# Two TensorE orders in a two-layer encoder: a differential head's outputs behind the next head's transposes, the first latent scores behind the latent values

## Chip, core and metric

The kernel runs on one core of one Trainium2 chip. Its engines work side by side, each through its own queue in order: TensorE (PE in the profile: matmuls, with the loads of their stationary operand shown apart as PEld), VectorE (DVE), ScalarE (ACT), GpSimd (POOL) and SyncE (SP), which issues the loads from memory. The metric is device time in microseconds; the time of a kernel is the median of several executions. One further execution is recorded by the hardware profiler, and all rows in this document are from such executions.

## What is computed

An encoder of two layers over 256 tokens with 2048 features, in f32. In each layer a differential attention and a latent attention stand side by side and are joined by gates; an output projection, a SwiGLU network and a gated embedding follow. The part that matters here, shortened:

```python
for i in range(DEPTH):                                   # 2 layers
    z = rmsnorm(x, g_mix[i]) @ w_in[i]
    dq, dk, dv, cq, ckv, kr, ga, gb = split(z)
    # differential attention: 8 heads, two softmax maps of 64 features each
    probs = softmax(einsum('bqhcd,bkhcd->bhcqk', rope(dq), rope(dk)) * 64 ** -0.5)
    od = (probs[:, :, 0] - lam * probs[:, :, 1]) @ dv
    y_diff = (rmsnorm(od, g_subln[i]) * (1 - lam_init)) @ w_branch_diff[i]
    # latent attention: 8 heads; queries, keys and values come from low-rank latents
    qf = rmsnorm(cq, g_q_latent[i]) @ w_q_up[i]           # 128 plain + 64 rotated features a head
    kvf = rmsnorm(ckv, g_kv_latent[i]) @ w_kv_up[i]       # 128 key + 128 value features a head
    probs = softmax((q_nope @ k_nope + rope(q_rope) @ rope(kr)) * 192 ** -0.5)
    y_mla = (probs @ v_mla) @ w_branch_mla[i]
    x = x + (sigmoid(ga) * y_diff + sigmoid(gb) * y_mla) @ w_out[i]
    x = x + swiglu(rmsnorm(x, g_ffn[i]))
    x = x + sigmoid(rmsnorm(x, g_ple[i]) @ w_ple_gate[i]) * (p[i] @ w_ple_in[i])
```

## The kernel before

Activations lie transposed, features on the 128 partitions and the 256 tokens along the free dimension, in 16 tiles. For accuracy, operands are split into a high and a low part: `split` does it for an activation (ScalarE copies the high part, VectorE subtracts, lines 250 and 251 with line 74), `piece` for up to 1024 columns of weights, which SyncE loads (line 180), ScalarE rounds to `whi` and VectorE subtracts to `wlo` (line 181). `emit` then runs, for each block of 128 input features, one matmul of `whi` with both parts of the activation (line 211, 512 columns) and one of `wlo` with its high part (line 215, 256 columns). This pair of matmuls is nearly all of the work. `joined` adds the two halves of a finished bank (ScalarE's copy on line 242, then VectorE). Weight splits have three buffers each, the loaded weights four, results of `joined` four (`a`).

PSUM, the matmuls' output memory, is given out in banks: four for projections and values (`ps_mm`, line 63), two for scores (`ps_s`, line 64), and two for all the rest (`ps_at`, line 65): transposes, head outputs, rotations, norms.

One differential head goes through these steps:

- `scores` (line 348): 12 matmuls into two score banks, one for each map;
- `exps` (lines 354 to 358): VectorE takes the maxima, ScalarE the exponentials with their sums (line 357), VectorE the reciprocals; then `diff_weights` scales and joins the two maps (lines 557 and 558) into the weights `E`;
- `turned` (line 366): four transposes of the weights into one bank, then ScalarE's copy of it to `wt` (line 368);
- `diff_out` (line 567): eight matmuls of `wt` with the values into another bank; ScalarE copies it out (line 570) and squares it twice for the norm (line 572). `settle` later scales the outputs of four heads, transposes them (line 582) and splits them.

`pipelined` lays the heads of one attention over each other and over other work. In turn h it takes a step of filling work, starts the scores of head h+1, traces head h's transposes, takes a second step, and then traces head h's outputs. For the differential heads the filling work is the generator `beside`: the queries and keys of later heads, the latent keys, the shared rotated key (with `rotated`, line 326), from head 6 on `settle` and the latent queries (`queries_up`, of which two of six pieces are rotated). What is left of it is taken after the loop, and then `values` computes the latent values (lines 399 to 401, into `mmv` banks). The latent heads go through `pipelined` too, with projections of the gates as filling work; `mla_weights` has their scores, also on line 348.

The code gives the work in an order, but the order in which each engine's queue gets it is planned when the program is built: the framework runs a model of the engines and hands each engine, at each modelled moment, the first traced instruction whose inputs and buffers are ready. Work traced later can so be drawn forward into a gap that the model sees. `tc.issue_after(x)` forbids it for one case: whatever is traced in its block on x's engine stays behind x. It orders a queue and adds no semaphore. `last_mm` holds the most recent line-401 matmul.

Of the kernel before, what the change touches and what calls it, by code (L numbers as in the profile page):

```python
# [19 lines left out]
P = 128  # L20
# [4 lines left out]
DH = 8  # L25
# [27 lines left out]
def encoder(ctx, tc, x, p, positions, cols, lams, wq, wk, wv, wcq, wckv, wkr, wga, wgb,  # L53
            w_q_up, w_kn, w_v, w_bd, w_bm, w_out, w_gate, w_up, w_down, w_pin, w_pg, rope_c, out):
    nc = tc.nc
    V, A, PE = nc.vector, nc.scalar, nc.tensor
# [13 lines left out]
    def bank(ps=ps_at, tag="at", name="at", shape=(P, 2 * T)):  # L70
        return ps.tile(list(shape), F32, tag=tag, name=name)

    def tt(o, a, b, op):
        return V.tensor_tensor(out=o, in0=a, in1=b, op=op)  # L74
# [4 lines left out]
    def ts(o, a, s1, s2, op0, op1=ALU.bypass):  # L79
        return V.tensor_scalar(out=o, in0=a, scalar1=s1, scalar2=s2, op0=op0, op1=op1)  # L80
# [29 lines left out]
    ident = const.tile([P, P], F32, name="ident")  # L110
# [83 lines left out]
    last_split, last_mm, chores, sq0, step = [], [], [], [], []  # L194
# [24 lines left out]
    def product(src, us, whole=False, inside=None):  # L219

        acc = bank(ps_mm, "mm", "mm")
        n = len(us)
        for a in range(0, n, PT):
            m = min(PT, n - a)
            hi, lo = piece(src[:, a * P : (a + m) * P], m)
            emit(acc, hi, lo, 0, us[a : a + m], a == 0, a + m == n, whole, inside and (inside[0] - a, inside[1]))
        return acc[:, :T] if whole else acc
# [10 lines left out]
    def joined(acc, o=None):  # L240
        t = scratch("join", 3)
        A.activation(t, acc[:, T:], AF.Copy)  # L242
        o = scratch("a", 4) if o is None else o
        tt(o, acc[:, :T], t, ALU.add)
        return o
# [74 lines left out]
    krs = [const.tile([P, 2 * T], F32R, name=f"kr{j}") for j in range(2)]  # L320
# [16 lines left out]
    def three(q, k):  # L337
        return [(q[:, :T], k[:, T:]), (q[:, T:], k[:, :T]), (q[:, :T], k[:, :T])]

    def scores(*maps):  # L340


        Ss = [bank(ps_s, "S", "S", (P, 2, T)) for _ in maps]
        for b in range(2):
            for j in range(len(maps[0])):
                for S, pairs in reversed(list(zip(Ss, maps))):
                    q, k = pairs[j]
                    PE.matmul(S[:, b, :], q[:, b * P : (b + 1) * P], k, start=j == 0, stop=j == len(pairs) - 1)  # L348
        return Ss

    def exps(S, E, scale):

        nm, sm, rs = (stat.tile([P, 2], F32, tag=t, name=t, bufs=4) for t in ("nm", "sm", "rsum"))
        V.tensor_reduce(out=nm, in_=S, axis=AX.X, op=ALU.max, negate=True)
        ts(nm, nm, scale, None, ALU.mult)
        for b in range(2):
            last_exp[0] = A.activation(E[:, b, :], S[:, b, :], AF.Exp, bias=nm[:, b : b + 1], scale=scale, accum_out=sm[:, b : b + 1])  # L357
        V.reciprocal(out=rs, in_=sm)
        return rs

    def turned(W, parts=False):

        tp = bank(shape=(P, 2, T))
        for kb in range(2):
            for b in range(2):
                PE.transpose(tp[:, kb, b * P : (b + 1) * P], W[:, b, kb * P : (kb + 1) * P], ident)  # L366
        wt = [tmp.tile([P, 2, T], F32R if parts else F32, tag="wt", name="wt", bufs=4) for _ in range(1 + parts)]
        A.activation(wt[0], tp, AF.Copy)
        if not parts:
            return wt[0]  # L370
        tt(wt[1], tp, wt[0].bitcast(F32), ALU.subtract)
        return wt
# [4 lines left out]
    def weights(tag="E", dt=F32):  # L377
        return tmp.tile([P, 2, T], dt, tag=tag, name=tag, bufs=2)

    last_exp = [None]  # L380
    ROPE16 = [(j + 8) if j < 8 else (j - 8) if j < 16 else j for j in range(32)]

    def values(src, us, load=None):
# [39 lines left out]
    for L in range(DEPTH):  # L423
# [43 lines left out]
        qn, kn, qr = [], [], ub[14:]  # L467
# [40 lines left out]
        def beside():  # L508

            for h in range(2, DH):  # L510
                if h < 6:
                    keys_up(2 * h - 4)
                elif h == 7:
                    rotated(joined(product(wkr[L, 0], ua)), crm, srm)
                yield
                queries_keys(h)
                yield
            settle(0)
            for n in (8, 0, 2, 10):
                queries_up(n)  # L520
                yield
            settle(4)
            for n in (4, 6):
                queries_up(n)
# [21 lines left out]
        fill = beside()  # L546
# [13 lines left out]

        def diff_out(h, W):
            wt = turned(W)
            yield
            o = bank()
            for b in range(2):
                for kb in range(2):
                    PE.matmul(o[:, b * P : (b + 1) * P], wt[:, kb, b * P : (b + 1) * P], head(vd, kb, h), start=kb == 0, stop=kb == 1)  # L567
            f = fa(h)
            od.append(f[:, 0, :])
            A.activation(od[h], o[:, :T], AF.Copy)  # L570
            for b in range(2):
                A.activation(f[:, 1, :P], od[h][:, b * P : (b + 1) * P], AF.Square, accum_out=ssd[:, 2 * h + b : 2 * h + b + 1])
# [9 lines left out]
                    PE.transpose(t[:, b * P : (b + 1) * P], o, ident)  # L582
                split(ods[h], t[:, :T], gsub[:, L : L + 1])

        def pipelined(weigh, put, heads, step):
            W = weigh(0)
            for h in range(heads):
                step()
                nxt = weigh(h + 1) if h + 1 < heads else None
                out = put(h, W)  # L590
                next(out)
                step()
                next(out, None)
                W = nxt

        pipelined(diff_weights, diff_out, DH, lambda: next(fill, None))
        for _ in fill:
            pass
        vm, = (v for v in values(w_v[L], ckv) if v is not None)
# [4 lines left out]

        def mla_weights(h):
            E = weights()
            S, = scores(three(qn[h], kn[h]) + three(qr[h // 2], krs[h % 2]))
            r = exps(S, E, MLA_SCALE)
            for b in range(2):
                ts(E[:, b, :], E[:, b, :], r[:, b : b + 1], None, ALU.mult)  # L610
            return E

        def mla_out(h, W):
            v = head(vm, slice(None), h)
            vs = weights("E1", F32R)
            vh, vl = vs[:, :, :P], vs[:, :, P:]
            A.activation(vh, v, AF.Copy)
            tt(vl, v, vh.bitcast(F32), ALU.subtract)
            wh, wl = turned(W, True)
            yield  # L620
            o = bank()
            for kb in range(2):
                for j, (a, b) in enumerate(((vh, wh), (vh, wl), (vl, wh))):
                    PE.matmul(o[:, :T], a[:, kb, :], b[:, kb, :], start=kb + j == 0, stop=kb + j == 3)  # L624
            split(oms[h], o[:, :T])

        pipelined(mla_weights, mla_out, MH, lambda: gate(wga, gate_a, next(todo)))


# [26 lines left out]
        for part, (f0, f1) in enumerate(FF_PARTS):  # L656
            for f in range(f0, f1):
# [6 lines left out]
                b = pre.pop(0) if pre else joined(product(w_up[L, f], ub))  # L664
# [128 lines left out]
```

## Time and profile before

| | us |
|---|---|
| median of 3 runs | 2852.53 (2852.42 to 2852.87) |
| the profiled execution, in all | 2853.86 |
| its span, first to last instruction | 2852.1 |
| differential heads, layers 1 and 2 | about 112 to 235 and 1525 to 1649 |
| latent heads | about 221 to 346 and 1634 to 1759 |

A row of the timeline has start, duration, engine, line, operation, output and inputs by their names in the program, the array's rows and columns for a matmul, shape, and how many were merged; in square brackets stands how long the engine was idle ahead of it and which instruction ended that. Matmuls overlap: the next starts before the last one's duration is over, so the step from start to start is what one costs. Tiles of `ps_at` are named `at`, those of the scores `S`. A row of busy times by stretch has the stretch, its length, then the busy time of PE, PEld, DVE, ACT and POOL, the granted clock, the share of time in which the DMA engines moved data, and GB/s. A row of waits has the waiting engine and line, the releasing one, us in total, how often, and the longest.

### The profile page before, as it was taken

Reading aid. Unit: us, or ns where it says so; the run is one execution under the profiler, and the core shown is the slowest. Engines: PE = TensorE matmul, PEld = TensorE weight load, DVE = VectorE, ACT = ScalarE, POOL = GpSimd, SP = SyncE. Lnnn points to the kernel's source line nnn. Section 1 sums busy time; section 2 is a strip of 40 time slices with the busy share of each in tenths; the row PEclk is TensorE's granted clock in tenths of the full one; section 3 lists DMA queues with packets and bytes.
Section 4 is the critical chain, followed back from the end, with each engine's and each line's share of the span. In section 5 each row is a group of like instructions: output and inputs, shape, how many; then the busy total and the mean of one; then the engine's idle time right before and its main releaser. Section 6 shows DMA issues by size and latency. Waiting matters only on the chain.

```text
span 2852.1 us, 43992 instructions
## 1 busy us (share of the span) xinstructions
PE 2832.8 (99%) x16750; PEld 2501.0 (88%) x16750; DVE 2064.8 (72%) x3529; ACT 1522.9 (53%) x2529; POOL 1.7 (0%) x9
## 2 busy tenths in 40 slices
PE   9999999999999999999999999999999999999998
PEld 7888888888888888888888888888888888888887
DVE  7898658776666666677859976687766666666776
ACT  6676545554444544455646755555544444444554
POOL 0000000000000000000000000000000000000000
PEclk9999999999999999999999999999999999999999
DMA  6544455555665566565555444555556655655654
GB/s 235 168 165 149 160 195 196 193 192 193 191 198 194 181 198 202 194 193 192 192 189 167 156 153 167 195 198 192 192 193 189 198 195 186 200 194 195 194 192 143
DMA packets 156020, 532.41 MB, mean 187 GB/s; under 512 B 16928, under 2 KB 23840, under 8 KB 155808
## 3 DMA queue, kind: packets, MB, share of 16 engines
q1 hardware_dynamic: 155376, 529.01, 56.4%
q8 instruction: 131, 2.15, 0.3%
q10 hardware_dynamic: 432, 0.59, 0.1%
q14 instruction: 81, 0.66, 0.1%
HBM read 527.43 MB, written 2.10 MB: 186 GB/s over the span
## 4 chain that ended last, share of the span: by engine, by line
PE 98%; DVE 1%; ACT 0%; DMA 0%; issue 0%; SPq 0%; DVEq 0%
PE mm L211 61%; PE mm L215 30%; PE S L348 1%; PE mmv L401 1%; PE mmv L400 1%; PE mmv L399 1%; PE at L366 1%; PE at L567 0%; PE at L624 0%; DVE wlo L74 0%; DMA w<-in_wv 0%; DVE a L74 0%; PE at L286 0%; DVE xT L74 0%; ACT E L357 0%
## 5 line engine op out<-in xcount | busy, mean ns | idle before, releaser
L181 ACT ACTIVATE whi<-w 128x1024 fp32r<-128x1024 f32 (+2 forms) x1029 | 1066.6, 1037 | 1252.1 <-issue 710.9
L74 DVE TENSOR_TENSOR wlo<-w,whi 128x1024 fp32r<-128x1024 f32 (+2 forms) x1029 | 1229.0, 1194 | 692.4 <-ACT whi L181 683.6
L211 PE MATMUL mm<-ub,whi 128*128 128x512 f32 x3952 | 1346.8, 389 | 0.0
L211 PE MATMUL mm<-ua,whi 128*128 128x512 f32 x3744 | 1281.2, 390 | 0.0
L215 PE MATMUL mm<-ub,wlo 128*128 128x256 f32 x3952 | 1092.4, 276 | 0.0
L215 PE MATMUL mm<-ua,wlo 128*128 128x256 f32 x3744 | 1036.6, 277 | 0.0
L211 PEld LDWEIGHTS mm<-ub,whi 128*128 128x128 f32 x3952 | 741.4, 188 | 152.6
L211 PEld LDWEIGHTS mm<-ua,whi 128*128 128x128 f32 x3744 | 702.0, 188 | 143.0
L215 PEld LDWEIGHTS mm<-ub,wlo 128*128 128x128 f32 x3952 | 741.8, 188 | 0.8
L215 PEld LDWEIGHTS mm<-ua,wlo 128*128 128x128 f32 x3744 | 702.9, 188 | 2.5 <-DVE wlo L74 0.8
L74 DVE TENSOR_TENSOR a<-mm,join 128x256 f32<-128x256 f32 x421 | 175.0, 418 | 0.2
L242 ACT ACTIVATE join<-mm 128x256 f32<-128x256 f32 x453 | 165.8, 367 | 4.4 <-PE mm L215 4.2
L74 DVE TENSOR_TENSOR xT<-xT,mm 128x256 f32<-128x256 f32 x256 | 106.8, 420 | 41.5 <-PE mm L215 37.7
L74 DVE TENSOR_TENSOR a<-a,row 128x256 f32<-128x256 f32 x207 | 87.7, 425 | 5.9
L74 DVE TENSOR_TENSOR a<-a 128x256 f32<-128x256 f32 x120 | 51.1, 426 | 4.1
L399 PE MATMUL mmv<-whi,ua 128*128 128x512 f32 x128 | 50.8, 398 | 3.0 <-ACT whi L181 3.0
L74 DVE TENSOR_TENSOR ua<-a,ua 128x256 fp32r<-128x256 f32 x120 | 50.2, 418 | 1.0 <-ACT ua L250 1.0
L400 PE MATMUL mmv<-whi,ua 128*128 128x512 f32 x128 | 50.8, 398 | 0.0
L250 ACT ACTIVATE ua<-a 128x256 fp32r<-128x256 f32 x120 | 48.3, 403 | 2.6 <-DVE a L74 2.6
L357 ACT ACTIVATE E<-S,nm 128x256 f32<-128x256 f32 x96 | 44.2, 470 | 6.9 <-DVE nm L80 6.9
L401 PE MATMUL mmv<-wlo,ua 128*128 128x512 f32 x128 | 46.9, 398 | 0.1
L74 DVE TENSOR_TENSOR ssq<-ssq,sq 128x256 f32<-128x256 f32 x97 | 40.6, 419 | 0.5 <-ACT sq L269 0.5
(154 smaller groups left out, 1160.5 us busy)
## 6 DMA issues: line engine op xcount, KB each, us to landing
w<-in_w_gate SPq DMA_DIRECT2D x176, 512.0 KB, 4.6
w<-in_w_up SPq DMA_DIRECT2D x176, 512.0 KB, 4.6
w<-in_w_down SPq DMA_DIRECT2D x128, 512.0 KB, 4.2
w<-in_wga SPq DMA_DIRECT2D x64, 512.0 KB, 3.7
w<-in_wgb SPq DMA_DIRECT2D x64, 512.0 KB, 4.2
w<-in_w_out SPq DMA_DIRECT2D x64, 512.0 KB, 4.5
w<-in_w_pg SPq DMA_DIRECT2D x64, 512.0 KB, 4.6
w<-in_w_down SPq DMA_DIRECT2D x64, 384.0 KB, 3.6
```

Source lines behind the costliest of these rows:

```text
L74: return V.tensor_tensor(out=o, in0=a, in1=b, op=op)
L181: last_split[:] = A.activation(hi[:, :m], w[:, :m], AF.Copy), tt(lo[:, :m], w[:, :m], hi[:, :m].bitcast(F32), ALU.subtract)
L211: lead = PE.matmul(acc, hi[:, s], u, start=start, stop=False)
L215: rest = PE.matmul(acc[:, T:], lo[:, s], u[:, :T], start=False, stop=stop)
L242: A.activation(t, acc[:, T:], AF.Copy)
L250: return A.activation(hi, src, AF.Copy), tt(lo, src, hi.bitcast(F32), ALU.subtract)
L348: PE.matmul(S[:, b, :], q[:, b * P : (b + 1) * P], k, start=j == 0, stop=j == len(pairs) - 1)
L357: last_exp[0] = A.activation(E[:, b, :], S[:, b, :], AF.Exp, bias=nm[:, b : b + 1], scale=scale, accum_out=sm[:, b : b + 1])
L366: PE.transpose(tp[:, kb, b * P : (b + 1) * P], W[:, b, kb * P : (kb + 1) * P], ident)
L399: PE.matmul(banks[b], xh, hi[:, s], start=a + j == 0, stop=False)
L400: PE.matmul(banks[b], xl, hi[:, s], start=False, stop=False)
L401: last_mm[:] = [PE.matmul(banks[b], xh, lo[:, s], start=False, stop=a + j == n - 1)]
```

## The change

Two orders on TensorE. With `late`, which the differential heads alone use, `pipelined` no longer traces head h's outputs in turn h after the second step. It keeps them, and in turn h+1 traces them behind head h+1's transposes, with an `issue_after` on the last of these, ahead of the second step. Head 7's outputs are traced after the loop, without it. `mla_weights` gets an `issue_after` on the last matmul of the values. No computation, buffer or load is added or taken away.

```diff
-                PE.transpose(tp[:, kb, b * P : (b + 1) * P], W[:, b, kb * P : (kb + 1) * P], ident)
+                last_turn[0] = PE.transpose(tp[:, kb, b * P : (b + 1) * P], W[:, b, kb * P : (kb + 1) * P], ident)
...
-        def pipelined(weigh, put, heads, step):
-            W = weigh(0)
+        def pipelined(weigh, put, heads, step, late=False):
+            W, before = weigh(0), None
             for h in range(heads):
                 step()
                 nxt = weigh(h + 1) if h + 1 < heads else None
                 out = put(h, W)
                 next(out)
-                step()
-                next(out, None)
+                if late:
+                    out, before = before, out
+                    if out:
+                        with tc.issue_after(last_turn[0].ins):
+                            next(out, None)
+                    step()
+                else:
+                    step()
+                    next(out, None)
                 W = nxt
+            if late:
+                next(before, None)

-        pipelined(diff_weights, diff_out, DH, lambda: next(fill, None))
+        pipelined(diff_weights, diff_out, DH, lambda: next(fill, None), True)
...
         def mla_weights(h):
             E = weights()
-            S, = scores(three(qn[h], kn[h]) + three(qr[h // 2], krs[h % 2]))
+            with tc.issue_after(last_mm[0].ins):
+                S, = scores(three(qn[h], kn[h]) + three(qr[h // 2], krs[h % 2]))
```

More of the change, by code (lines that the diff above doesn't have):

```diff
@@ L378, in weights @@
         return tmp.tile([P, 2, T], dt, tag=tag, name=tag, bufs=2)
-    last_exp = [None]
+    last_exp, last_turn = [None], [None]
     ROPE16 = [(j + 8) if j < 8 else (j - 8) if j < 16 else j for j in range(32)]
```

## The prediction

> **What bounds the kernel now.** I read the page first, then the busy times by stretch, then TensorE's own waits, then the timeline around the one wait that is left.
>
> ```profile
> span 2852.1 us, 43992 instructions
> PE 2832.8 (99%) x16750; PEld 2501.0 (88%) x16750; DVE 2064.8 (72%) x3529; ACT 1522.9 (53%) x2529; POOL 1.7 (0%) x9
> ...
> 0.00:12.40 12.40, 8.30 (x31) 6.58 (x32) 4.16 (x8) 6.51 (x11) 1.70 (x9) 1.00 0.76 248
> 12.40:2836.00 2823.60, 2821.87 (x16710) 2492.74 (x16709) 2052.40 (x3500) 1515.07 (x2516) 0.00 (x0) 1.00 0.57 187
> 2836.00:2852.10 16.10, 2.59 (x13) 1.70 (x12) 8.28 (x22) 1.34 (x3) 0.00 (x0) 0.59 0.34 130
> ...
> PE S L348 <- ACT E L357: 1.7, 2, 0.8
> ```
>
> TensorE sets the time. Between the start-up (to 12.4 us) and the final norm (from 2836 us), neither of which the diff touches, it is busy for 2821.87 of 2823.60 us: 1.73 us idle. The last row, from the waits of TensorE alone, names nearly all of it: two waits, 1.7 us together, of a score matmul (line 348) for ScalarE's exponentials (line 357). Whatever the diff moves, every moved matmul still has to run, so a gain can only come out of these 1.73 us and out of slivers between matmuls. A loss has no such limit.
>
> ```profile
> 219.39 0.28 PE L215 MATMUL mm<-ub,wlo 128*128 128x256 f32 x1
> 219.50 0.59 PE L326 MATMUL at<-a,rc 128*128 128x256 f32 x2
> 219.93 0.60 PE L366 MATMUL at<-ident,E 128*128 128x128 f32 x4
> 221.37 0.62 PE L348 MATMUL S<-fb,fa 128*128 128x256 f32 x3 [0.83 <-ACT E L357]
> ...
> 1634.39 0.62 PE L348 MATMUL S<-fb,fa 128*128 128x256 f32 x3 [0.84 <-ACT E L357]
> ...
> 220.76 0.47 ACT L357 ACTIVATE E<-S,nm 128x256 f32<-128x256 f32 x1
> 221.11 0.20 ACT L357 ACTIVATION_READ_ACCUMULATOR E<-S,nm 128x1 f32 x1
> ...
> 221.71 0.41 DVE L74 TENSOR_TENSOR sh<-at,sin_m 128x256 f32<-128x256 f32 x1
> ```
>
> This is the wait in the timeline, once in each layer. The scores are the first of the latent heads. They need a score bank (two exist, line 64) that the last differential head still occupies: its second exponential ends at 221.11 + 0.20 = 221.31, and the matmul starts 0.06 later. TensorE issues in order, so the projection matmuls behind it stand still too. The transposes of differential head 6 are directly ahead of the hole.
>
> **The change, part by part.** Nothing is added or removed in work. Two things are moved on TensorE.
>
> The first is the block of eight output matmuls of a differential head (line 567), in 16 heads.
>
> ```profile
> 134.57 0.39 PE L211 MATMUL mm<-ua,whi 128*128 128x512 f32 x1
> ...
> 134.91 0.39 PE L211 MATMUL mm<-ua,whi 128*128 128x512 f32 x1
> 135.14 1.05 PE L567 MATMUL at<-vals,wt 128*128 128x128 f32 x8
> 135.95 0.36 PE L215 MATMUL mm<-ua,wlo 128*128 128x256 f32 x1
> 136.15 0.39 PE L211 MATMUL mm<-ua,whi 128*128 128x512 f32 x1
> ```
>
> From start to start a pair of projection matmuls takes 134.91 - 134.57 = 0.34 us; the pair that has the block inside takes 136.15 - 134.91 = 1.24. The block costs 0.90, of which eight matmuls at 0.11 (0.81 us from 135.14 to 135.95 with the last one overlapped) are about 0.89. Standing alone therefore costs about 0.01, and putting it behind four transposes saves that 14 times (head 7 of each layer has no following transposes): **-0.14 us**. I take nothing for scores and transposes, whose own order stays.
>
> Each block moves later, to the next head's transposes, so TensorE reaches the work in between 0.9 us sooner. That helps only if the operands are there. The tightest place I found is behind the first head's block.
>
> ```profile
> 136.80 0.16 DVE L80 TENSOR_SCALAR nm<-nm 128x2 f32<-128x2 f32 x1
> 139.45 0.23 DVE L80 TENSOR_SCALAR rsum<-rsum,neg_lam 128x2 f32<-128x2 f32 x1
> 140.20 1.23 DVE L74 TENSOR_TENSOR wlo<-w,whi 128x1024 fp32r<-128x1024 f32 x1 [0.52 <-ACT whi L181]
> ...
> 136.23 0.39 ACT L570 ACTIVATE fa<-at 128x256 f32<-128x256 f32 x1 [1.64 <-PE at L567]
> 137.00 0.47 ACT L357 ACTIVATE E<-S,nm 128x256 f32<-128x256 f32 x1
> 139.10 1.06 ACT L181 ACTIVATE whi<-w 128x1024 fp32r<-128x1024 f32 x1
> ...
> 141.49 0.38 PE L215 MATMUL mm<-ua,wlo 128*128 128x256 f32 x1
> 141.71 0.40 PE L211 MATMUL mm<-ua,whi 128*128 128x512 f32 x1
> ```
>
> VectorE's half of a weight split ends at 140.20 + 1.23 = 141.43, and TensorE takes it 0.06 us later, at 141.49, in a matmul that is followed after 0.22 instead of the usual 0.11. So 0.9 us sooner would be waited for, up to 0.84 a layer, if the split stayed. It need not: ScalarE now waits 1.64 us, in order, for the very outputs that leave (line 570), with the exponentials and the first half of that split queued behind. The exponentials can't gain (the maxima they need come at 136.80 + 0.16 = 136.96, and the first starts at 137.00), but the outputs' evictions leave the queue, and VectorE can start as soon as its last small operation is over (139.45 + 0.23 = 139.68), 0.52 sooner. That leaves 0.9 - 0.06 - 0.52 = 0.32 a layer: bounds 0 and 0.84, I take 0.3, so **+0.6 us** in two layers.
>
> The second part holds the first latent scores back until the latent values' last matmul. That takes the 0.83 and 0.84 us away, **-1.67 us**, unless something else is late there. What stands in the hole then is either the next projection pair or the outputs of head 5, 0.90 us, now due directly behind head 6's transposes. What is late next is head 7.
>
> ```profile
> 204.70:228.20 23.50, 22.66 (x151) 19.95 (x150) 22.67 (x56) 19.80 (x55) 0.00 (x0) 1.00 0.40 136
> ...
> 221.82 0.28 PE L348 MATMUL S<-kr,ub 128*128 128x256 f32 x1
> 222.88 1.05 PE L567 MATMUL at<-vals,wt 128*128 128x128 f32 x8
> 224.24 0.52 PE L348 MATMUL S<-fb,fa 128*128 128x256 f32 x3
> 224.59 0.28 PE L348 MATMUL S<-kr,ub 128*128 128x256 f32 x1
> 226.08 0.40 PE L348 MATMUL S<-kr,ub 128*128 128x256 f32 x2
> 226.32 0.52 PE L348 MATMUL S<-fb,fa 128*128 128x256 f32 x3
> 226.67 0.64 PE L348 MATMUL S<-kr,ub 128*128 128x256 f32 x4
> 228.18 0.27 PE L366 MATMUL at<-ident,E 128*128 128x128 f32 x1
> ...
> 225.36 0.48 DVE L77 SCALAR_TENSOR_TENSOR E<-E,rsum,E 128x256 f32<-128x256 f32 x1
> ```
>
> Ahead of head 7's transposes (228.18) stand, with the four at 221.37 and 221.82, 17 latent scores at 0.12 (226.32 - 226.08 for two): 2.0 us. They leave; so does head 6's output block (0.90 at 222.88), while head 5's comes in and fills the hole. TensorE gets to these transposes about 2.0 + 0.9 us sooner, at 225.3, and the weights they turn are ready at 225.36 + 0.48 = 225.84. Reading that as a new wait of 0.5 us is the upper bound, because projection pairs can go ahead of it; 0 is the lower. I take 0.2 a layer, **+0.4 us**.
>
> The waits that the change adds are of this kind: the outputs now stand behind transposes that wait for VectorE, with projection pairs behind them, whose banks ScalarE and VectorE empty. The latent scores add no semaphore, only an order within TensorE; the latent heads that come later have the gate projections as cover. Weight loads (SyncE's queue) keep their order, and splits are far enough ahead of the values:
>
> ```profile
> 225.75 1.21 DVE L74 TENSOR_TENSOR wlo<-w,whi 128x1024 fp32r<-128x1024 f32 x1
> ...
> 235.43 0.39 PE L399 MATMUL mmv<-whi,ub 128*128 128x512 f32 x1
> ```
>
> The second piece of the values is split by 226.96 and first used at 235.43. So 3 us sooner on TensorE starves nothing there.
>
> **Sum.** -0.14 + 0.6 - 1.67 + 0.4 = -0.8 us. Against the profiled span that is 2852.1 - 0.8 = 2851.3. The runs' median is 2852.53, 0.43 above that span (the profiled execution itself took 2853.86 in all), so I forecast **2851.7 us**, 0.03% faster. A change of under 0.2%, 5.7 us, is about what a measurement of this kernel can tell from none. Bounds of the terms: best -0.14 + 0 - 1.67 + 0 = -1.8; worst, with 0.84 and 0.5 twice, -0.14 + 1.68 - 1.67 + 1.0 = +0.9. The forecast's own range is 2850.7 to 2853.4.
>
> **Rivals.** (1) *A bank takes the place of the wait.* The pool for transposes and outputs has two banks (line 65). At 219.50 the rotation (line 326) takes one, at 219.93 the transposes the other. VectorE reads the rotation until 221.71 + 0.41 = 222.12. Outputs directly behind the transposes, whose own issue ends at about 219.93 + 4 x 0.11 = 220.37, would wait 1.75 us, against 0.83 now. That is 0.9 worse a layer instead of 0.83 better: 2 x 0.92 - 0.14 + 0.6 + 0.4 = +2.7, 2855.2 us. For it: VectorE is busy for 22.67 of 23.50 us there and can't hurry. Against it: the order only forbids going earlier, and other work may be planned in between.
>
> (2) *The cover is gone.* This is the slower one, in the stretch from 204.7 to 228.2 us and its twin. If VectorE, not TensorE, sets when that stretch ends (22.67 of 23.50 us busy), the 17 scores and the output block that leave it are not time won there but time added behind it, where TensorE is full: 2.0 + 0.9 = 2.9 us a layer, **+5.8 us, 2858.3**. It decides from the point where the joins and exponentials in that stretch come no sooner although TensorE does; half of it gives +2.9, 2855.4. Against it stands that the splits are well ahead and that VectorE idles little but is not what TensorE waits for in any row, the one hole aside. A larger hole could also cost clock. The granted clock is 1.00 through the stretch with 0.83 us holes and 0.59 in the last 16.10 us, where TensorE has only 2.59 us of work. The Trainium skill ("TensorE: Matmul & The Clock Gate", Part 1) says that an idle window of some 3.4 us halves the clock for about as long; by that rule one hole that grows so far would add an estimated 1.7 us a layer to this rival, and the last stretch agrees with it while no hole in the changed places is long enough to test it.
>
> (3) *It doesn't do what it says.* The planner that sets each engine's order leaves the outputs late enough and puts something else into the hole that waits as long: no change, 2852.5. For it: the order is planned on modelled times, and the hole itself shows that plan and chip differ.
>
> (4) *More than the waits.* TensorE's weight loads are busy for only 2492.74 of 2823.60 us, so a planner with another order might seem to have 12% to win. The steady 0.34 us from pair to pair, unbroken but for the blocks, speaks against it; I price it at -6 us, 2846.5, only to have the side covered.
>
> **How the numbers follow.** Forecast 0.53; rival 1, and half of rival 2, 0.23; rival 2 in full or beyond 0.15; rival 3 0.06; rival 4 0.03. Within 0.2% are the forecast, rival 1 and rival 3: 0.82. Slower is rival 2 in full, 0.15; faster is rival 4, 0.03. The range reaches from below the forecast's own (2850.7, less 0.7 for the slivers I didn't price) to the far side of rival 1 and the half of rival 2, 2850.0 to 2857.2, and leaves out rivals 2 and 4 in full, 0.18.
>
> **What would show it.** Right: no wait of line 348 for line 357 in TensorE's waits; the outputs of head h-1 within a microsecond behind the transposes of head h; no latent score before the last values' matmul; ScalarE's 1.64 us wait ahead of line 570 gone; TensorE idle for under 1 us between 12.4 and 2836 us. Wrong, by rival 1: outputs that wait for VectorE's rotation. By rival 2: several waits of TensorE for VectorE between 204 and 240 us, 2 us or more a layer, with the stretch ending no sooner. A forecast that fails everywhere would show the projections at another step than 0.34 us.

## The result, and the profile after

| | before | after |
|---|---|---|
| median of 22 runs each, us | 2853.00 (2852.38 to 2855.11) | 2857.53 (2856.35 to 2859.73) |
| ratio, with its 95% interval | | 1.0015 (1.0009 to 1.0020) |
| span of the profiled execution, us | 2852.1 | 2854.6 |

The change makes the kernel 4.5 us slower. The forecast was 0.8 us faster, and the range ended at 2857.2. The prediction took 0.2% for about the least that can be told from no change; the interval here is about 0.06% to either side, so the 0.15% is clear of it.

These are the views of the changed kernel that answer to those of before: the page's first lines, the busy times by stretch, and TensorE's waits between 12.4 and 2838 us (waiting engine and line, releaser, us in total, times, longest).

```profile
span 2854.6 us, 43996 instructions
PE 2834.1 (99%) x16750; PEld 2501.1 (88%) x16750; DVE 2064.4 (72%) x3529; ACT 1525.3 (53%) x2529; POOL 1.7 (0%) x9
...
12.40:2838.50 2826.10, 2821.90 (x16702) 2491.70 (x16701) 2050.28 (x3497) 1515.84 (x2513) 0.00 (x0) 1.00 0.57 186
...
PE mmv L399 <- ACT vals L405: 1.9, 2, 1.0
PE mm L211 <- DVE a L74: 1.4, 2, 0.7
PE mm L211 <- DVE nm L80: 0.4, 2, 0.2
PE at L326 <- ACT wt L368: 0.2, 1, 0.2
```

The wait of a score for ScalarE's exponentials is gone, as meant. In its place stand four others, and TensorE idles 4.20 us in the long middle part, where it idled 1.73. All of this idle time lies in two stretches, one in each layer (2.11 and 2.09 us). Here is layer 1 before the change, and then layers 1 and 2 after it:

```profile
204.00:240.00 36.00, 35.16 (x226) 31.00 (x225) 32.52 (x82) 29.23 (x83) 0.00 (x0) 1.00 0.39 132
```

```profile
204.00:240.00 36.00, 33.89 (x205) 28.73 (x204) 31.62 (x83) 27.57 (x74) 0.00 (x0) 1.00 0.42 141
...
1617.00:1653.00 36.00, 33.91 (x206) 28.75 (x205) 31.89 (x77) 28.00 (x75) 0.00 (x0) 1.00 0.39 132
```

Two things are to be seen. VectorE is not fuller than before (31.62 us against 32.52), which speaks against a stretch that simply ran out of VectorE. And TensorE's idle time grows by only 1.27 us a layer, which doesn't make 4.5 us. The remainder hides in the durations: a matmul's row lasts 0.39 us in a step of 0.23, so it covers part of the wait behind it. It is better to compare steps from start to start. This is TensorE in the changed kernel, at the five places where a step is too long:

```profile
212.63 0.59 PE L326 MATMUL at<-a,rc 128*128 128x256 f32 x2
213.91 0.47 PE L211 MATMUL mm<-ub,whi 128*128 128x512 f32 x1 [0.69 <-DVE a L74]
...
219.68 1.05 PE L567 MATMUL at<-vals,wt 128*128 128x128 f32 x8
220.49 0.49 PE L211 MATMUL mm<-ub,whi 128*128 128x512 f32 x1
...
221.31 0.47 PE L211 MATMUL mm<-ub,whi 128*128 128x512 f32 x1 [0.22 <-DVE nm L80]
...
226.90 0.60 PE L366 MATMUL at<-ident,E 128*128 128x128 f32 x4
227.34 1.06 PE L567 MATMUL at<-vals,wt 128*128 128x128 f32 x8
228.54 1.13 PE L326 MATMUL at<-a,rc 128*128 128x256 f32 x4
229.76 1.16 PE L567 MATMUL at<-vals,wt 128*128 128x128 f32 x8
231.88 0.50 PE L399 MATMUL mmv<-whi,ub 128*128 128x512 f32 x1 [0.96 <-ACT vals L405]
```

An output block alone takes 0.81 us (219.68 to 220.49), a rotation (x2 in its row) 0.43 (219.50 to 219.93 before), a projection pair 0.34. So the lost time is: behind the rotation 1.28 - 0.43 = 0.85; at the pair of 220.49, 0.82 - 0.34 = 0.48; behind head 6's outputs 1.20 - 0.81 = 0.39; behind the two rotations 1.22 - 0.86 = 0.36; behind head 7's outputs 2.12 - 0.81 = 1.31. Together 3.4 us. Before, the one hole cost 221.37 - 219.93 - 0.44 = 1.0. I did the same for every step between 204 and 245 us (and 1617 to 1658), each against what the same step takes undisturbed: 1.77 and 1.78 us lost before, 3.92 and 3.95 after. The difference, 2.15 + 2.17 = 4.3 us, is the slowdown. Everywhere else between 15 and 2825 us the two kernels agree within 0.2 us a stretch. A second way needs no undisturbed steps: two matmuls of line 286, which belong to norms and stand ahead of and behind all the heads of layer 1, start 509.11 us apart before (108.74 and 617.85) and 511.24 after (106.94 and 618.18), and in layer 2 the distance grows by 2.24. The profiled spans differ by only 2.5 us because the start-up of the kernel before (0 to 15 us) lost 6.5 us in its profiled execution and the other 4.7.

What are these steps waiting for? VectorE and then ScalarE in the changed kernel:

```profile
212.21 1.22 DVE L74 TENSOR_TENSOR wlo<-w,whi 128x1024 fp32r<-128x1024 f32 x1 [0.56 <-ACT whi L181]
213.35 0.41 DVE L74 TENSOR_TENSOR a<-mm,join 128x256 f32<-128x256 f32 x1
...
226.81 2.45 DVE L74 TENSOR_TENSOR wlo<-w,whi 128x1024 fp32r<-128x1024 f32 x2 [0.46 <-ACT whi L181]
229.28 0.42 DVE L74 TENSOR_TENSOR sh<-at,sin_m 128x256 f32<-128x256 f32 x1
```

```profile
230.95 0.38 ACT L570 ACTIVATE fa<-at 128x256 f32<-128x256 f32 x1 [1.27 <-PE at L567]
231.23 1.08 ACT L405 ACTIVATE vals<-mmv 128x512 f32<-128x512 f32 x2
```

- At 213.91 a pair takes a projection bank that VectorE's join empties at 213.35 + 0.41 = 213.76. The join stood in VectorE's queue behind a weight split.
- At 229.76 head 7's outputs take the bank that the first rotation had; VectorE read it until 229.28 + 0.42 = 229.70, again behind splits.
- At 231.88 the values' second half needs the banks of the first, which ScalarE copies out (line 405, two in 1.08 us). These copies stand in ScalarE's queue behind the eviction of head 7's outputs (line 570), for which ScalarE waited. Before the change, the second half started at 235.43, and ScalarE's copies of the first half only at 235.68. So there it had other banks, and did not wait for the copies at all.

That is a reading of rows. The runs test it.

### The profile page after: what moved, and what is told of

Its sections match the earlier page's. It is cut to its first block, busy times and chain, and to the rows that moved or that the text cites. A ratio compares the mean times of both kernels' runs of the same rounds, so it can differ in the third digit from the quotient of the medians.

```text
span 2854.6 us, 43996 instructions
## 1 busy us (share of the span) xinstructions
PE 2834.1 (99%) x16750; PEld 2501.1 (88%) x16750; DVE 2064.4 (72%) x3529; ACT 1525.3 (53%) x2529; POOL 1.7 (0%) x9
## 3 DMA queue, kind: packets, MB, share of 16 engines
q8 instruction: 131, 2.15, 0.3%
## 4 chain that ended last, share of the span: by engine, by line
PE 98%; ACT 1%; DVE 1%; DMA 0%; SPq 0%; issue 0%; DVEq 0%
PE mm L211 61%; PE mm L215 31%; PE S L348 1%; PE mmv L401 1%; PE mmv L399 1%; PE mmv L400 1%; PE at L366 1%; PE at L567 0%; PE at L635 0%; ACT whi L181 0%; DVE wlo L74 0%; DMA w<-in_wv 0%; PE at L286 0%; DVE xT L74 0%; PE at L277 0%; ACT E L357 0%
```

## Experiments

Each run was timed in five rounds, with runs of the kernel before beside it; "against before" is the difference of the two medians. Lost time is the sum explained above, in us, as a mean of the two layers, for the stretch from 204 us on; the column behind it is 2 x (lost - 1.775).

| run | us | against before | ratio (95%) | lost | from lost |
|---|---|---|---|---|---|
| the change | 2857.53 | +4.5 | 1.0015 (1.0009 to 1.0020) | 3.93 | +4.3 |
| e1 part 1 alone | 2856.47 | +3.2 | 1.0012 (1.0003 to 1.0021) | 3.27 | +3.0 |
| e2 part 2 alone | 2856.12 | +2.8 | 1.0012 (1.0003 to 1.0021) | 3.47 | +3.4 |
| e3 score bank for head 7 | 2856.25 | +3.0 | 1.0011 (1.0002 to 1.0019) | 3.12 | +2.7 |
| e4 part 2, split held | 2854.67 | +0.8 | 1.0002 (0.9994 to 1.0011) | 2.37 | +1.2 |
| e5 part 2, scores between halves | 2854.80 | +0.9 | 1.0003 (0.9994 to 1.0012) | 2.45 | +1.4 |
| e6 both | 2852.81 | -1.1 | 0.9996 (0.9987 to 1.0004) | 1.57 | -0.4 |
| e7 heads 0 to 3 late | 2850.45 | -3.5 | 0.9989 (0.9980 to 0.9998) | 0.63 | -2.3 |
| e8 part 1, split held | 2857.15 | +4.1 | 1.0014 (1.0005 to 1.0022) | 3.57 | +3.6 |
| e9 whole change, mended | 2853.59 | +0.5 | 1.0002 (0.9993 to 1.0011) | 1.96 | +0.4 |
| e10 heads 0 to 2 late | 2853.73 | +0.7 | 1.0004 (0.9995 to 1.0012) | 1.76 | 0.0 |
| e11 heads 0 to 4 late | 2851.23 | -1.9 | 0.9995 (0.9986 to 1.0004) | 0.66 | -2.2 |
| e12 scores behind outputs 6 | 2851.94 | -1.6 | 0.9995 (0.9986 to 1.0004) | 1.09 | -1.4 |

The last column follows the measured one within 1.2 us, in thirteen kernels. So the stretch is where nearly all of the change lives, and lost time in it is a good ruler, finer than the timing. It leaves out what happens elsewhere, which matters for e7 and e10, as shown below.

### Which part costs: e1, e2, e3

e1 has the outputs moved and leaves the latent scores as before; e2 the other way round. e3 is the whole change, with head 7's outputs in a score bank instead of one of the two banks that rotations and transposes share:

```diff
-            o = bank()
+            o = bank(ps_s, "S", "S") if h == DH - 1 else bank()
```

> The changed kernel with the first part alone: outputs behind the next head's transposes, latent scores free to go early again. Theory B (the cover is gone: the latent scores that left the stretch had filled TensorE's waits, so the second part costs the time): the scores fill the waits again, TensorE idles under 0.9 us a layer between 204 and 240 us, 2851.5 to 2853.5 us. Theory A (crowding: outputs of heads 6 and 7, both late rotations and the values meet at the end of the stretch, and bank and queue order there cost the time, so the first part does it): idle stays near 2.1 us a layer, 2856.5 to 2858 us.

> The kernel before with the second part alone: latent scores behind the values' last matmul, outputs where they were. Theory B: nothing fills the stretch, TensorE idles 2 us or more a layer between 204 and 240 us, 2856 to 2858 us. Theory A: the two waits of 0.83 us go and nothing comes in their place, 2851 to 2852.7 us.

> The changed kernel, with head 7's outputs written to one of the two score banks, which are free by then, instead of the banks that transposes and rotations share. Theory A: head 7's outputs no longer wait for VectorE's reading of the rotations, ScalarE gets to the values' banks sooner, the wait of line 399 for line 405 (0.96 us a layer) goes, and the time falls by about 2 us to 2855 to 2856. Theory B: a wait of the same length stands elsewhere in the stretch, 2857 to 2858 us.

Both parts cost, 3.2 and 2.8 us, so neither theory that puts the loss on one of them stands. Together they cost 4.5 and not 6.0; the wait of 0.96 us for the copies of the values, which stands in e1 and in e2, comes but once when both are there. The score bank brings 0.8 us a layer less lost time in the stretch: with it head 7's outputs no longer wait for a rotation's bank, and the copies come sooner. But 2856.25 lies between what the two theories said, and the wait for the copies, which theory A expected to go, is still there. This is TensorE in e3:

```profile
229.61 0.70 PE L326 MATMUL at<-a,rc 128*128 128x256 f32 x2 [0.16 <-ACT wt L368]
230.15 1.05 PE L567 MATMUL S<-vals,wt 128*128 128x128 f32 x8
...
232.16 0.50 PE L399 MATMUL mmv<-whi,ub 128*128 128x512 f32 x1 [0.53 <-ACT vals L405]
```

The copies are waited for 0.53 us now, not 0.96.

e1 holds a surprise. It has latent scores between the halves of the values (228.91 to 235.45, with head 7's transposes, head 6's outputs and two rotations among them), and the 0.96 us wait is there all the same:

```profile
235.45 1.05 PE L567 MATMUL at<-vals,wt 128*128 128x128 f32 x8
237.47 0.50 PE L399 MATMUL mmv<-whi,ub 128*128 128x512 f32 x1 [0.96 <-ACT vals L405]
```

Head 7's outputs are the last thing ahead of the second half, and the copies come only behind their eviction. What covers the wait is therefore work between head 7's outputs and the second half, not scores anywhere between the halves.

### Part 2 taken apart: e4, e5, e6

In e2 the scores have left the hole of 0.83 us, and the hole has grown. TensorE and VectorE of e2:

```profile
218.91 0.60 PE L366 MATMUL at<-ident,E 128*128 128x128 f32 x4
220.92 0.47 PE L211 MATMUL mm<-ub,whi 128*128 128x512 f32 x1 [1.41 <-ACT wt L368]
...
219.14 1.23 DVE L74 TENSOR_TENSOR wlo<-w,whi 128x1024 fp32r<-128x1024 f32 x1
220.35 0.43 DVE L74 TENSOR_TENSOR a<-mm,join 128x256 f32<-128x256 f32 x1
```

The row says that the pair waits for ScalarE's copy of the settled weights. The times say otherwise: the join ends at 220.35 + 0.43 = 220.78, and a projection bank is then free. Ahead of the join stands the split of the values' first piece, which TensorE uses only from 226.0 on. And the pair starts 220.92 - 218.91 = 2.01 us behind the start of head 6's transposes, just as before the change (221.94 - 219.93), although four scores have left the gap. e4 keeps a list of the joins and holds that split behind the fifth-last of them; nothing else is changed against e2:

```diff
-        tt(o, acc[:, :T], t, ALU.add)
+        joins.append(tt(o, acc[:, :T], t, ALU.add))
...
+                with ExitStack() as stack:
+                    if behind and half == 0:
+                        stack.enter_context(tc.issue_after(behind.ins))
-                hi, lo = piece(src[half][:, a * 512 : (a + m) * 512], 4 * m)
+                    hi, lo = piece(src[half][:, a * 512 : (a + m) * 512], 4 * m)
...
-        vm, = (v for v in values(w_v[L], ckv) if v is not None)
+        vm, = (v for v in values(w_v[L], ckv, None, joins[-5]) if v is not None)
```

> Part 2 alone (the latent scores behind the values, head outputs as before), and VectorE's split of the latent values' first weight piece is held until behind the fifth-last projection join. Theory (projection banks): the 1.41 us hole of TensorE at the projection pair near 220.9, which the waits put to the settled weights, is really a projection bank that waits for VectorE's join, and the join stands behind that 1.23 us split. The hole then shrinks to 0.3 or less in each layer, and 2 x 1.1 us come back from part 2 alone's 2856.1: 2853.9, with the 0.96 us wait for the values' copies unchanged. Rival (the inferred releaser is right: the settled weights, or head 7's transposes are late): the hole stays at 1.4 and the time at 2856.1.

TensorE, VectorE and ScalarE of e4:

```profile
219.84 0.60 PE L366 MATMUL at<-ident,E 128*128 128x128 f32 x4
220.71 0.47 PE L211 MATMUL mm<-ub,whi 128*128 128x512 f32 x1 [0.27 <-DVE a L74]
...
220.14 0.42 DVE L74 TENSOR_TENSOR a<-mm,join 128x256 f32<-128x256 f32 x1
...
222.53 1.23 DVE L74 TENSOR_TENSOR wlo<-w,whi 128x1024 fp32r<-128x1024 f32 x1
...
222.02 0.61 ACT L368 ACTIVATE wt<-at 128x512 f32<-128x512 f32 x1
```

The join goes first, the hole shrinks from 1.41 to 0.27, and the time against the kernel before goes from +2.8 to +0.8 us. The theory had said 2853.9, so a little less comes back than expected, but the rival's 2856.1 is out. The bank was the cause. ScalarE's copy of the weights was not: in e4 it comes at 222.02, 1.3 us after the pair that was said to wait for it.

e5 is e2 with the scores held behind the last matmul of the values' first half only:

```diff
             if not half:
+                mid_mm[:] = last_mm
...
-            with tc.issue_after(last_mm[0].ins):
+            with tc.issue_after(mid_mm[0].ins):
                 S, = scores(three(qn[h], kn[h]) + three(qr[h // 2], krs[h % 2]))
```

> Part 2 alone, but the latent scores come behind the last matmul of the values' first half in place of the last of all. Theory (lost cover): the values' second half waits 0.96 us in each layer for ScalarE's copies of the first half's banks, because the scores that stood between the halves are gone; with scores there again that wait is 0.1 or less, the hole of 1.41 at the projections stays, and the time is 2856.1 - 1.9 = 2854.2. Rival (the time goes by the number of scores left ahead of the values, in the 204 to 228 stretch): nothing changes there, 2856.1.

Of TensorE's two waits in e2's stretch this one is left, and the 0.96 us wait for the values' copies is gone:

```profile
PE mm L211 <- ACT wt L368: 1.4, 1, 1.4
```

The second half still starts 2.02 us behind the start of head 7's outputs (232.37 to 234.39, as 230.08 to 232.10 in e2), but nine scores now stand behind these outputs and fill the time.

e6 has both edits.

> Part 2 alone with both edits: the split held behind the fifth-last join, and the scores behind the values' first half. If both holes are separate, and each is what the theory says, TensorE's loss in the stretch falls to about 1.2 us a layer, against 1.77 before the change: 2853.3 - 2 x 0.5 = 2852.2, the same as before or faster. Rival (the stretch is held by VectorE's total work, which was busy all but 0.8 us of it, and not by its order): one hole only takes the place of the other, and it stays at 2855 or above.

One short wait is left in the stretch of e6, 0.3 us of a projection pair for a join (line 211 for line 74), and the lost time (1.57) is below that of before.

Part 2's cost is thus two separate holes, each gone or nearly so with its own edit, and the sum of both edits is nearly the effect of the two together: 3.47 - 1.10 - 1.02 = 1.35 against 1.57 measured.

### Part 1: e8, e9

The same idea for the hole at 213.91 (at 214.46 in e1): the split that stands ahead of the join, which belongs to the last pair of latent queries, is held behind it.

```diff
-            for acc in pair(w_q_up[L, n : n + 2], cq):
+            for acc in pair(w_q_up[L, n : n + 2], cq, joins[-5] if n == 6 else None):
```

> Part 1 alone, and VectorE's split of one weight piece of the 256-column projections (the last pair's, which starts at 212.75 in part 1 alone) is held behind the join that stands after it. Theory (projection banks): that split makes the join late, the join frees the bank, and TensorE's 0.69 us hole at the pair near 214.4 is this bank; the hole goes, the 0.96 us wait for the values' copies stays, TensorE's loss in the stretch falls from 3.27 to about 2.6 a layer, and the time from part 1 alone's 2856.5 to about 2855.1. Rival (VectorE has too much work there, whatever its order): the hole reappears at one of the next pairs and the time stays at 2856.5.

TensorE and VectorE of e8, where the line numbers of this part of the code are 3 higher than in the change:

```profile
212.92 0.59 PE L329 MATMUL at<-a,rc 128*128 128x256 f32 x2
213.16 0.58 PE L211 MATMUL mm<-ub,whi 128*128 128x512 f32 x1
...
221.90 0.47 PE L211 MATMUL mm<-ub,whi 128*128 128x512 f32 x1 [1.45 <-DVE nm L80]
...
215.87 1.21 DVE L74 TENSOR_TENSOR wlo<-w,whi 128x1024 fp32r<-128x1024 f32 x1
217.67 1.21 DVE L74 TENSOR_TENSOR wlo<-w,whi 128x1024 fp32r<-128x1024 f32 x1
221.34 0.41 DVE L74 TENSOR_TENSOR a<-mm,join 128x256 f32<-128x256 f32 x1
```

The rival's case: the hole at the first place is gone, and one of 1.45 us stands 8 us later, where the held split and the next one (215.87 and 217.67) are now both ahead of a join (221.34). One split put back is not enough here, since it comes due somewhere. e9 therefore holds this one and the values' first piece, and puts the scores between the halves, in the whole change:

> The whole change, with three edits that only give orders: the split of the last projection pair held behind a join (as in the run before), the split of the values' first piece held behind a join, and the latent scores behind the values' first half in place of their last matmul. Theory (the loss is made of the bank waits behind the two splits, 0.69 and 0.2 to 0.4 us, and the values' copies that nothing covers, 0.96 us): the three holes go, TensorE's loss falls from 3.93 a layer to about 1.9, and the time from 2857.5 to 2853.5. Rival (the merged output blocks themselves crowd two rotation banks and four buffers whatever the splits do): the loss stays at 2.8 or more, 2855.3 or above.

All that is left of waits in its stretch:

```profile
PE mm L211 <- DVE nm L80: 0.3, 1, 0.3
PE S L351 <- ACT E L360: 0.2, 1, 0.2
```

2853.59 us, within 0.1 of the theory, with every output block still behind the next head's transposes as in the change. So 4 of the 4.5 us are not the price of the moved blocks themselves: they go when VectorE's splits and joins, and the latent scores, get another order. The three edits were not taken apart here. In e9 the second half of the values starts at 236.94, ahead of the first copy at 237.29, so it has other banks again and doesn't need the cover.

### Which heads: e7, e10, e11, e12

These move the outputs of the first heads alone (4 in e7, 3 in e10, 5 in e11), with the latent scores as before; the later heads have their outputs where they were.

```diff
-                if late:
+                if late and h < 4:
```

> Part 1 alone for heads 0 to 3 (their outputs directly behind the next head's transposes); heads 4 to 7 have their outputs in their old place, the latent scores too. Theory: moving the outputs of a head costs only where banks are short, that is with heads 5 to 7 beside the 256-column projections: the stretch from 204 on loses 1.8 us a layer as before the change, and the time is 2853.3 (2852.8 to 2853.8). Rival (each moved output block costs a little, or the tight split behind head 0's outputs at 141.5 costs its 0.6 a layer): about half of part 1's 3.2 us, 2854.5 or more, with the loss in the stretch from 105 to 204.

> Part 1 alone for heads 0 to 2, one head fewer than the run that came to 2850.45. The order planned for TensorE from head 6 on is then again that of before the change (four latent scores ahead of the three projection pairs behind head 7's transposes). Theory (the gain of the run with heads 0 to 3 is not worth of the moved outputs, but lies in the order that the planner happened to give the latent scores and the joins in the stretch): loss 1.8 a layer in the stretch, 2853.3 (2852.8 to 2853.8). Rival (each early head's moved output block saves something): 2851.2 or below.

> Part 1 alone for heads 0 to 4, one head more. TensorE's planned order has the latent scores in blocks behind projection pairs, and outputs 5 ahead of the settled heads. Theory (what costs is that the projections start 0.9 us sooner when head 5's outputs have left, and the crowd at the end; head 4's outputs cost nothing): loss between 0.65 and 1.8 a layer in the stretch, 2850.5 to 2853.3. Rival (the loss grows with each head moved): 2854 or more.

e7 came out better than expected, 3.5 us faster than the kernel before. In its stretches TensorE never idles (36.00 of 36.00 us in layer 2 too):

```profile
204.00:240.00 36.00, 36.00 (x235) 32.16 (x234) 33.96 (x85) 28.57 (x78) 0.00 (x0) 1.00 0.41 133
```

And this is its order on TensorE, projection pairs left out, with the join and the split on VectorE:

```profile
220.17 0.60 PE L366 MATMUL at<-ident,E 128*128 128x128 f32 x4
220.52 0.48 PE L211 MATMUL mm<-ub,whi 128*128 128x512 f32 x1
...
223.36 1.05 PE L567 MATMUL at<-vals,wt 128*128 128x128 f32 x8
224.17 0.60 PE L348 MATMUL S<-fb,fa 128*128 128x256 f32 x3
...
219.91 0.43 DVE L74 TENSOR_TENSOR a<-mm,join 128x256 f32<-128x256 f32 x1
...
220.32 1.23 DVE L74 TENSOR_TENSOR wlo<-w,whi 128x1024 fp32r<-128x1024 f32 x1
```

TensorE never idles in e11's stretches either. e10, with one head fewer, gains nothing there and still has the score's wait of 0.8 us in each layer. So in the stretch it isn't each moved block that pays. With four or five heads moved, the planned order differs near the end: projection pairs, not latent scores, stand directly behind these transposes (at 220.52, without a wait), and VectorE's join at 219.91 goes ahead of the split. In e7 the first scores come at 224.17, behind head 6's outputs; in e11 they come at 222.89, ahead of these outputs, and the loss is as small, so that place is not needed for the gain. e12 sets e7's order with two `issue_after`, and moves no output block: the scores held behind head 6's last output matmul, the split behind a join as in e4.

> No output of a differential head is moved (part 1 is out). The first latent scores are held behind head 6's outputs, and not behind the values' matmuls, and VectorE's split of the values' first piece is held behind the fifth-last projection join. Theory (what made the runs with heads 0 to 3 and 0 to 4 faster than before is the place of the first latent scores behind head 6's outputs together with the joins ahead of the split, and not the moved outputs): no wait of a score for its bank, at most 0.3 us at the pair near 220.7, the values' copies covered by the scores between the halves; loss 0.9 to 1.1 a layer in the stretch against 1.77, 2853.2 - 2 x 0.8 = 2851.6. Rival (the early heads' moved outputs are what gains): 2853.2, loss 1.7.

2851.94 us and 1.09 us lost, in line with the theory: 0.69 of the 1.15 us a layer that e7 gains in the stretch need no moved outputs. e12's timing alone doesn't exclude no change (its interval reaches 1.0004); its lost time does the telling. The fastest of all is e7, the only one whose whole interval lies below 1.

e7 and e10 also gain outside the stretch. The two matmuls of line 286 around the heads of layer 1, 509.11 us apart before, are 507.51 apart in e7, 508.65 in e10, 508.01 in e11 and 508.35 in e12, and layer 2 gains the same within 0.1 us. So e7 gains 1.6 us a layer, of which the stretch holds 1.15; e10 gains 0.46, though its stretch gains nothing; e11 gains 1.1 and e12 0.76, about what their stretches hold. That explains why e7 is 1.2 us faster than its lost time says. e10's measured +0.7 doesn't show its gain, but its interval (0.9995 to 1.0012) doesn't exclude it. Moving the first three or four heads gains about 0.45 us a layer there, and moving five does not; no run takes this part apart. e7 was measured in one set of runs, and the greater part of its gain hangs on where a planned order happens to fall, so I would take e12's two explicit orders into the kernel and not e7's head count.

## Why the prediction was wrong

- **"-0.14 us" for merged blocks.** Not seen. Between 105 and 204 us, 3.75 us was lost before and 3.85 after, layer 2 alike (3.81, 3.93). Not every block merged either: five of seven a layer start 0.11 us behind the last transpose, but head 4's outputs start 4.0 us and head 5's 2.5 us behind it. With fewer heads moved, e7 and e10 gain about 0.45 us a layer outside the stretch; whether by merging is not shown.
- **"+0.6 us" behind the first head's outputs.** Nothing. In the changed kernel ScalarE rounds this weight piece at 134.58, ahead of the exponentials (135.55), where it had come behind them (139.10 against 137.00). VectorE's split of it ends at 136.16 + 1.20 = 137.36, and TensorE takes it at 138.78, 1.4 us later. The lower bound, 0, was right.
- **"-1.67 us, unless something else is late there ... What is late next is head 7."** This is the step that failed, for part 2. The two waits did go. What was late next was not head 7's transposes, which run at 226.90 without any wait (so the +0.4 term is nil as well), but the projection bank for the very next pair. These are VectorE and TensorE before the change:

```profile
220.17 1.22 DVE L74 TENSOR_TENSOR wlo<-w,whi 128x1024 fp32r<-128x1024 f32 x1
221.37 0.42 DVE L74 TENSOR_TENSOR a<-mm,join 128x256 f32<-128x256 f32 x1
...
221.94 0.41 PE L211 MATMUL mm<-ub,whi 128*128 128x512 f32 x1
```

  The score's wait ended at 221.37, and VectorE's join, which frees that bank and stood behind a split, at 221.37 + 0.42 = 221.79, with the pair at 221.94. So 0.83 us of waiting for a score bank lay inside a wait for another bank, and four scores were done on the way at no cost. Taking them out could win nothing there: in e2 the pair comes as late as before, the hole is 1.41 us instead of 0.83, and the four scores are paid for elsewhere. With the 0.96 us for the values' copies, part 2 costs 2.8 us where this term was -1.67.
- **"So 3 us sooner on TensorE starves nothing there."** This is the step that failed for part 1, which costs 3.2 us alone (e1) where its two terms made +0.46. I looked at when operands are ready (weight splits 2 us and more ahead) and put the banks at nothing: the text names the projections' banks, which ScalarE and VectorE empty, and has no term for them. By the times in the rows, every new wait in e1, e2 and the change is for a bank, and e4, e5 and e9 take the larger ones away with orders alone. Head 5's outputs, which I had put into the hole, come only at 219.68, 2.9 us behind the start of head 6's transposes (216.78).
- **Rival 1** named the right kind of thing, outputs that wait for VectorE's rotation, at the wrong head. Head 5's outputs, of which it spoke, come at 219.68 without a wait; head 7's do wait, for 0.36 us where I had 1.75, and e3 takes it away.
- **Rival 2** had the right sign and, with 2.9 to 5.8 us, the size that holds 4.5. Its mechanism was half right at most. Missing cover is part of it: in e2 the copies are waited for 0.96 us, and scores put back between the halves of the values hide that (e5). But it wasn't cover that was lost; before the change the second half didn't need the copies, and e1 has scores between the halves and waits as long. Why the second half gets the first half's banks in these kernels and not before is not shown. And VectorE's total work was not the limit; it is busy for less than before in the stretch, and e9 wins 4 us back with the same work in another order. The range ended at 2857.2 because I took only half of that rival into it.
- The granted clock stays at 1.00 in both stretches after. No hole of TensorE in these stretches is longer than 1.45 us in any run, so the rule of the Trainium skill ("TensorE: Matmul & The Clock Gate", Part 1) about idle windows of some 3.4 us was not put to the test.

What stays open: part 1's first hole. The split ahead of the join at 213.35 waits 0.56 us for ScalarE's rounding (in e1 too), and ScalarE's rounding for a matmul of line 211, so perhaps for a buffer that TensorE frees. No run tests the links of this chain one by one, and e8, which moves that split, only moves the hole.

## What to carry to other kernels

A wait that ends may stand inside another one that ends a little later: before counting a removed wait as won, look up for the instruction behind it when each of its resources comes free, banks as well as operands. On an engine that both prepares operands and empties banks, preparation done early is not free; here a 1.23 us split that was needed 6 us later held up a join that was needed at once. Work with no deadline, such as the latent scores here, can serve as cover between two uses of the same banks; it has to stand directly ahead of the second use, behind whatever delays the emptying, as e5 has it and e1 has not.

## What the runs showed that I had not expected

- The releaser that the profile infers can be wrong by engine: the 1.41 us were put down to ScalarE's copy of the weights, and went to 0.27 when a VectorE split was put later. In e8 a bank's wait was put down to a small VectorE operation next to the join.
- TensorE's busy time understates a loss: 1.27 us more idle a layer, against 2.15 us lost from start to start. It also hides what can be won: before the change TensorE was idle for 1.73 us and lost 3.55 from start to start, and e7 gains 3.5 us, where the prediction saw no more than the idle time and slivers to gain.
- The profiled start-up (0 to 15 us) lost between 4.7 and 7.1 us from one kernel to the next, though none of the edits touches it. That is more than most of the effects here, so spans of single profiled executions could not have ranked these kernels; steps inside the stretch could.
